# Two conv-gated FFNs: five column groups of seven block products instead of four, each beside a narrow group, and two weight sums made by DMA

## The chip, the cores and the metric

The kernel runs on one core of one Trainium2 chip. The metric is device microseconds of one execution, as the median of some runs of the same program. Five engines of the core work side by side, each through its own queue of instructions in order: TensorE (PE, with its weight loads shown apart as PEld), VectorE (DVE), ScalarE (ACT), GpSimd (POOL) and SyncE (SP, which here only issues DMAs). They wait for each other through semaphores. TensorE reads SBUF and writes PSUM, which this kernel uses as eight banks of 512 fp32 columns per partition.

## The reference

Two decoder layers over 256 positions of width 2048. Each has a token mixer (layer 0: dilated attention in three groups; layer 1: stick-breaking attention on a shared K/V; both beside cross-attention into 256 memory tokens) and then a gated MLP with a causal depthwise convolution of width 3 on the gate branch. The change touches the MLP alone:

```python
def _conv_ffn(h, w_up, w_conv, b_conv, w_down):      # w_up 2048 x 11264, w_down 5632 x 2048
    u = h @ w_up
    gate, val = jnp.split(u, 2, axis=-1)
    gp = jnp.pad(gate, ((0, 0), (CONV_WIDTH - 1, 0), (0, 0)))
    acc = b_conv + gp[:, CONV_WIDTH - 1:CONV_WIDTH - 1 + S] * w_conv[CONV_WIDTH - 1]
    for j in range(CONV_WIDTH - 1):
        acc = acc + gp[:, j:j + S] * w_conv[j]
    return (jax.nn.silu(acc) * val) @ w_down
...
    f = _conv_ffn(_rmsnorm(x, norms[2]), w_up, w_conv, b_conv, w_down)
    return x + _rmsnorm(f, norms[3])
```

## The kernel before

**Arithmetic.** Every fp32 matrix is split into a high and a low part of the type fp32r: ACT casts the high part (`hi`, L557), DVE subtracts it to get the low part (`lo`, L558). A product is then three matmuls, hi·hi, lo·hi and hi·lo (`mm3`). Weights come as pieces of 1 MB (128 x 2048) into the ring `raw` (3 buffers), and each half of a piece takes a buffer of the rings `whi` and `wlo` (4 each).

**The FFN** (`ffn`, called for layer 0 and layer 1) walks over the 5632 columns of the gate and of the value in 11 groups of 512, each group twice 512 columns of `w_up`.

- A *narrow* group is eight tiles of 128 columns (`ws_pair`, `ws_tile`): weights stationary, the activations h moving, 16 matmuls of 512 columns (L135, L138) and 16 of 256 (L136) into one bank `ps_g`. An ACT copy (L139) and a DVE add (L140) empty the bank. Then the gate is scaled by the row factor R (L743), convolved (ACT L712, DVE L715), put through SiLU (L717), multiplied with the value (L727), and split (L253, L254).
- A *wide* group (`wide`, groups 2, 4, 6 and 8) makes gate and value together as a 2 x 2 block product with seven products instead of eight (a Strassen-Winograd form): token halves by rows, even and odd k-tiles, gate and value columns. It runs over eight *units* of k. One unit needs a 1 MB piece of weights, four sums of its quarters (DVE L590, L591, L592), splits of both, and 7 x 3 matmuls of 512 columns into seven banks that stay open over all units: products 1, 2, 6, 7 in `ps_g`, products 3, 4, 5 in `ps_s`. One bank of `ps_s` is left. Sums of the activations (`sums_of_h`, its step `make`) are made once per FFN. The results come out with tokens on partitions, and `turned` turns them by sixteen transposes (L758).
- The *down* product of a group is four pieces, each 24 matmuls (`as_mm`). In the wide stage one down piece is put beside the seven products of each unit: its first half ahead of products 1, 2, 3, its second half between them and products 7, 5, 6, 4. It uses the one free `ps_s` bank twice, and ACT alone empties it (L701). The partial results go by accumulating DMA from the POOL queue into `yout` in DRAM (L689).

**What sets the order.** Instructions are scheduled by a planner, except those under `pin` while `self.pinned` is true: each of those is kept behind the one that was written before it on its engine. Inside `wide`, PE, ACT and DVE thus follow the program text. `later(n, fn)` hangs a step on the n-th weight piece from now.

The activation rings that matter are `sh` (11 buffers of 4 KB per partition) and `qk` (5). The tile `x` serves as the residual and, during the wide groups, as room for the split sums (`forms`); the residual waits in DRAM (`xout`).

Of the kernel before, what the change touches and what calls it, by code (L numbers as in the profile page):

```python
# [36 lines left out]
WIDE = (2, 4, 6, 8)  # L37
# [8 lines left out]
class Body:  # L46
    def __init__(self, ctx, tc, a):
        self.tc, self.nc, self.a = tc, tc.nc, a
        self.sb = ctx.enter_context(tc.tile_pool(name="sb", bufs=1))
        self.todo = []  # L50
        self.pinned = False
        self.psp = ctx.enter_context(tc.tile_pool(name="ps", bufs=1, space=bass.MemoryType.PSUM))
        self.outside = ctx.enter_context(tc.tile_pool(name="outside", bufs=1, space=bass.MemoryType.DRAM))
# [28 lines left out]
    def step(self):  # L82
        if self.todo:
            for fn in self.todo.pop(0):
                fn()

# [54 lines left out]

    def ws_pair(self, src, h, out=None, before=None, R=None):
# [25 lines left out]
    def as_piece(self, banks, src, lhs, pi, cuts=1, between=None):  # L168
        self.step()
        parts = self.piece(src[pi], cuts, between=between and between[0])  # L170
# [23 lines left out]
    def rstd(self, ss):  # L194
# [5 lines left out]
        nc.gpsimd.tensor_tensor(r, v, self.mhalf[:, 0:n], op=ALU.pow)  # L200
        return r
# [50 lines left out]
    def split_heads(self, src, hi, lo):  # L252
        self.nc.scalar.copy(hi, src)  # L253
        self.nc.vector.tensor_sub(lo, src, hi.bitcast(F32))  # L254
# [281 lines left out]
    def sums_of_h(self, h):  # L536
# [3 lines left out]
        nc = self.nc  # L540
        s = self.sb.tile([P, KT // 2, 4, 2, P], F32R, name="h1", tag="h1", bufs=1)

        def make(i):
            a, d = self.pairtile(), self.pairtile().rearrange("p a (b t) -> p (a b) t", b=2)
            hh = h[2][:, 2 * i:2 * i + 2, :, :].bitcast(F32)
            nc.vector.tensor_add(a, hh[:, :, 0, :], hh[:, :, 1, :])
            a1, a2 = a[:, :, 0:P], a[:, :, P:S]
            nc.vector.tensor_add(d[:, 0, :], a2[:, 0, :], a2[:, 1, :])
            nc.vector.tensor_sub(d[:, 1, :], d[:, 0, :], a1[:, 0, :])
            nc.vector.tensor_sub(d[:, 2, :], a1[:, 0, :], a2[:, 0, :])  # L550
            nc.vector.tensor_sub(d[:, 3, :], a1[:, 1, :], d[:, 1, :])
# [8 lines left out]
    def wide(self, src, h, s, forms, r, downs):  # L560
# [9 lines left out]
        pin, sub = self.pin, nc.vector.tensor_sub  # L570
# [11 lines left out]
        def load(u):  # L582
            raw = self.sb.tile([P, 2048], F32, name="raw", tag="raw", bufs=3)
            nc.sync.dma_start(raw, src[u])
            return raw

        def sums(raw):

            d, e = self.sh([P, 1024]), self.sh([P, 1024])
            pin(sub(d, raw[:, 1024:], raw[:, 512:1536]))  # L590
            pin(sub(half(e, 1), half(raw, 3), half(d, 0)))  # L591
            pin(sub(half(e, 0), half(raw, 0), half(e, 1)))  # L592
            return d, e

        def plain(raw):
# [3 lines left out]
            self.split(*(half(f, 0) for f in fb), half(raw, 3))  # L599
            return fa, fb  # L600

        summed = [[forms[:, 2 * i + j, :] for j in range(2)] for i in range(2)]
        def split_sums(t):
            for of, parts in zip(t, summed):
                self.split(*parts, of)

        raw = load(0)
        t = sums(raw)
        split_sums(t)
        d = downs[0]()  # L610
        next(d)
        f = plain(raw)
        self.pinned = True
        for u in range(n):
            more = u + 1 < n
            next(d)
            if u:
                split_sums(t)
            next(d)
# [4 lines left out]
            if more:  # L624
                raw = load(u + 1)
                t, f = sums(raw), plain(raw)
            next(d)
# [8 lines left out]
            d = after  # L636
        a = [self.sc([P, 512]) for _ in range(2)]
        g0, v1 = self.sc([P, 512]), self.sc([P, 512])
        rt = [r[:, t:t + 1] for t in range(2)]
        for t in range(2):  # L640
            pin(nc.scalar.activation(a[t], ps[1], AF.Copy, scale=rt[t]))  # L641

        def add(out, i, t, to):
            pin(nc.vector.scalar_tensor_tensor(out, ps[i], rt[t], to, op0=ALU.mult, op1=ALU.add))

        add(g0, 2, 0, a[0])
        add(a[1], 7, 1, a[1])
        add(a[0], 6, 0, a[0])
        add(a[1], 6, 1, a[1])
        add(v1, 5, 1, a[1])  # L650
        add(a[0], 5, 0, a[0])
        add(a[0], 3, 0, a[0])
        add(a[1], 4, 1, a[1])
        self.pinned = False
        return (g0, a[1]), (a[0], v1)

    def ffn(self, layer, h, each, filler=None, done=None, late=None):
# [3 lines left out]

        def rms():
            with self.tc.issue_after(self.last_hi.ins):
                rx = self.x_rstd()
            R.append(rx)
# [11 lines left out]
        for i in range(KT // 2):  # L677
            self.later(2 * i + 1, lambda i=i: make(i))
# [3 lines left out]
        ss = self.sums(2)  # L682
        acts = {}

        def out(g, c, part):
            if g == 0:
                nc.gpsimd.dma_start(yout[c], part)
            else:
                nc.gpsimd.dma_start(yout[c], part, accum_op=ALU.add)  # L689

        def down(g, c):


            parts = self.piece(dn[c, g])
            y = self.sh([P, 1024])
            yield
            for t in range(2):
                b = self.bank("s")
                self.as_mm([b, b], parts, acts[g], 0, (t,))
                yield  # L700
                self.pin(nc.scalar.copy(y[:, t * 512:(t + 1) * 512], b))  # L701
                if t:
                    out(g, c, y)
                else:
                    yield

        def conv(p, ga):
            c = self.pairtile()
            for j in range(2):
                ft = 2 * p + j  # L710
                w = [self.cols[:, cv + i * NFT + ft:cv + i * NFT + ft + 1] for i in range(4)]
                nc.scalar.activation(c[:, j, :], ga[:, j, :], AF.Identity, scale=w[2], bias=w[3])  # L712
# [361 lines left out]
```

## Time and profile before

| | |
|---|---|
| median of 3 runs | 2205.47 us (2205.09 to 2206.46) |
| profiled execution | 2204.65 us, span of the profile 2202.9 us |
| clock granted to TensorE | 0.999 |
| DMA | 470.65 MB, mean 214 GB/s |
| wide groups | 64 units (two FFNs x 4 groups x 8) |

Times in the profile are in microseconds from the start of the span. A line such as L558 is a line of the kernel; a helper's line stands for all its callers, so tiles (`raw`, `sh`, `qk`) tell the stages apart. In a timeline a matmul's length runs to its modelled end; the distance between two starts is what it costs the engine. Names stand as out<-in.

### The profile page before, as it was taken

What the parts mean: (1) busy time and instruction counts of PE and PEld (TensorE: products, weight loads), DVE (VectorE), ACT (ScalarE), POOL (GpSimd) and SP (SyncE); (2) the same over time, 40 slices, a digit from 0 to 9 for tenths busy, and PEclk for the clock granted to TensorE, in tenths of its full rate; (3) what the DMA queues carried; (4) which work ended last, traced back from release to release, by engine and by line L of the source; (5) the groups of instructions that cost most, each with busy time, mean ns of one, the idle gap of its engine ahead of it and who ended that gap; (6) DMA issues with size and microseconds to landing.
All of it is one profiled execution on the core that took longest, in us unless ns stands there. A gap on an engine that the chain in (4) does not pass through costs nothing.

```text
span 2202.9 us, 29043 instructions
## 1 busy us (share of the span) xinstructions
PE 2188.7 (99%) x11106; PEld 1848.0 (84%) x11106; DVE 1713.0 (78%) x2215; ACT 1297.1 (59%) x1838; POOL 79.9 (4%) x122
## 2 busy tenths in 40 slices
PE   9999999999999999999999999999999999999998
PEld 7888888888888888888888888878888888888886
DVE  6566767898888989886674667568989889898766
ACT  7545656666565666665464545456666666666543
POOL 0000000000000000010000000000000000001000
PEclk9999999999999999999999999999999999999999
DMA  8755556557586786886555444555685868768753
GB/s 316 268 181 179 184 172 210 191 210 249 191 259 211 235 238 210 251 302 208 188 172 191 144 173 171 183 195 194 223 254 190 259 196 247 229 213 257 278 191 133
DMA packets 73708, 470.65 MB, mean 214 GB/s; under 512 B 8416, under 2 KB 8800, under 8 KB 23008
## 3 DMA queue, kind: packets, MB, share of 16 engines
q1 hardware_dynamic: 60768, 418.45, 55.2%
q0 software_dynamic: 12800, 50.34, 9.5%
q8 instruction: 87, 1.43, 0.3%
q14 instruction: 53, 0.43, 0.0%
HBM read 428.91 MB, written 39.85 MB: 213 GB/s over the span
## 4 chain that ended last, share of the span: by engine, by line
PE 98%; issue 1%; DVE 1%; DMA 0%; ACT 0%; SPq 0%; POOLq 0%; POOL 0%; DVEq 0%; ACTq 0%
PE ps_g L135 28%; PE ps_g L118 26%; PE ps_s L118 23%; PE ps_g L136 15%; PE ps_g L138 2%; PE ps_s L758 1%; PE ps_s L240 1%; DMA raw<-in_wmv_dram 0%; PE ps_s L291 0%; PE ps_s L318 0%; DVE wlo L558 0%; PE ps_s L397 0%; PE ps_s L354 0%; PE ps_s L455 0%; PE ps_s L415 0%
## 5 line engine op out<-in xcount | busy, mean ns | idle before, releaser
L558 DVE TENSOR_TENSOR wlo<-raw,whi 128x1024 fp32r<-128x1024 f32 (+1 forms) x758 | 881.3, 1174 | 328.8 <-ACT whi L557 316.2
L557 ACT CAST whi<-raw 128x1024 fp32r<-128x1024 f32 (+1 forms) x758 | 760.5, 1012 | 395.2 <-PE ps_g L118 166.5
L135 PE MATMUL ps_g<-h,whi 128*128 128x512 f32 x2640 | 943.0, 399 | 0.2 <-DVE h L230 0.2
L136 PE MATMUL ps_g<-h,wlo 128*128 128x256 f32 x2816 | 761.0, 280 | 0.0
L135 PEld LDWEIGHTS ps_g<-h,whi 128*128 128x128 f32 x2640 | 495.8, 188 | 114.6 <-ACT sc L641 1.9
L136 PEld LDWEIGHTS ps_g<-h,wlo 128*128 128x128 f32 x2816 | 531.6, 189 | 14.2
L118 PE MATMUL ps_s<-whi,sh 128*128 128x512 f32 x1088 | 336.6, 391 | 0.0
L118 PE MATMUL ps_g<-whi,h 128*128 128x512 f32 x816 | 254.1, 392 | 0.9 <-ACT whi L557 0.9
L118 PEld LDWEIGHTS ps_s<-whi,sh 128*128 128x128 f32 x1088 | 204.4, 188 | 45.2
L118 PE MATMUL ps_s<-wlo,sh 128*128 128x512 f32 x544 | 214.3, 394 | 0.4 <-DVE wlo L558 0.4
L139 ACT COPY qk<-ps_g 128x256 f32<-128x256 f32 x160 | 59.4, 371 | 209.1 <-PE ps_g L138 209.0
L118 PEld LDWEIGHTS ps_g<-whi,h 128*128 128x128 f32 x816 | 152.7, 188 | 34.8 <-ACT whi L557 1.3
L118 PE MATMUL ps_g<-whi,sh 128*128 128x512 f32 x560 | 174.8, 393 | 0.0
L558 DVE TENSOR_TENSOR x<-sh,x 128x1024 fp32r<-128x1024 f32 x128 | 156.2, 1223 | 18.5 <-ACT x L557 11.4
L118 PE MATMUL ps_g<-wlo,h 128*128 128x512 f32 x408 | 160.2, 393 | 0.2
L557 ACT CAST x<-sh 128x1024 fp32r<-128x1024 f32 x128 | 134.4, 1050 | 17.4 <-PE ps_s L118 16.4
L701 ACT COPY sh<-ps_s 128x512 f32<-128x512 f32 x128 | 74.4, 581 | 106.0 <-PE ps_s L118 106.0
L118 PEld LDWEIGHTS ps_g<-whi,sh 128*128 128x128 f32 x560 | 104.8, 188 | 22.1
L118 PEld LDWEIGHTS ps_s<-wlo,sh 128*128 128x128 f32 x544 | 102.2, 188 | 23.2 <-DVE wlo L558 1.3
L140 DVE TENSOR_TENSOR qk<-ps_g,qk 128x256 f32<-128x256 f32 x160 | 67.3, 420 | 55.2 <-ACT qk L139 54.4
L118 PE MATMUL ps_g<-wlo,sh 128*128 128x512 f32 x280 | 109.8, 392 | 0.0
L118 PE MATMUL ps_g<-x,h 128*128 128x512 f32 x384 | 109.2, 392 | 0.0
(173 smaller groups left out, 1953.9 us busy)
## 6 DMA issues: line engine op xcount, KB each, us to landing
raw<-in_up_dram SPq DMA_DIRECT2D x112, 1024.0 KB, 5.0
raw<-in_dn_dram SPq DMA_DIRECT2D x88, 1024.0 KB, 4.8
raw<-in_uw_dram SPq DMA_DIRECT2D x64, 1024.0 KB, 7.2
yout<-sh POOLq DMA_DIRECT2D x64, 512.0 KB, 8.4
raw<-in_wqk_a_dram SPq DMA_DIRECT2D x24, 1024.0 KB, 4.8
raw<-in_wo_b_dram SPq DMA_DIRECT2D x16, 1024.0 KB, 4.9
raw<-in_wv_a_dram SPq DMA_DIRECT2D x12, 1024.0 KB, 4.9
raw<-in_wv_b_dram SPq DMA_DIRECT2D x12, 1024.0 KB, 4.8
```

The costliest lines, as they stand in the source:

```text
L118: mm = lambda *o, **k: self.pin(self.nc.tensor.matmul(*o, **k))
L135: mm(b, whi[:, ks], both, start=kt == 0, stop=False)
L136: mm(b[:, 0:S], wlo[:, ks], one, start=False, stop=False)
L138: mm(b, whi[:, ks], both, start=False, stop=True)
L139: nc.scalar.copy(out, b[:, S:])
L140: nc.vector.tensor_add(out, b[:, 0:S], out)
L240: self.nc.tensor.transpose(b[:, k * S + t * P:k * S + (t + 1) * P], self.x[:, t, kt * P:(kt + 1) * P], self.ident)
L557: self.pin(self.nc.scalar.copy(hi, of))
L558: self.pin(self.nc.vector.tensor_sub(lo, of, hi.bitcast(F32)))
L701: self.pin(nc.scalar.copy(y[:, t * 512:(t + 1) * 512], b))
L758: nc.tensor.transpose(b[:, j * S + t * P:j * S + (t + 1) * P], of[t][:, f:f + P], self.ident)
```

## The change

Groups 1, 3, 5, 7 and 9 of each FFN are wide now, five instead of four. Beside the products of each unit stands one tile of the *narrow* group behind it (`ws_beside`, `beside`: eight tiles beside eight units), where a down piece stood. The two down products of earlier groups (`downs`) come between wide groups as a stage of their own. What belongs to the narrow tiles (gate, convolution, product, splits) is put into a list (`behind_this`) of which one step is taken at each of two places of a unit (`catch_up`). Of the four weight sums of a unit, two that lie in one buffer `d` are made by DMA: a load of two quarters, and on top of it an accumulating DMA from the POOL queue that adds the fourth quarter to both. DVE makes the other two. The signs of the activation sums change with it, and `turned` goes through an ACT copy. Three of the eight `make` steps move into the first wide group. The last three down products keep their place at the end, with the wide group's own last.

```diff
-WIDE = (2, 4, 6, 8)
+WIDE = (1, 3, 5, 7, 9)
...
+    def catch_up(self, n=1):
+        while self.behind and n:
+            self.behind.pop(0)()
+            n -= 1
...
+    def ws_beside(self, out, src, h, done=None):
+        parts = self.piece(src)
+        yield
+        b = self.bank("s")
+        mm = lambda *o, **k: self.pin(self.nc.tensor.matmul(*o, **k))
+        for half, (whi, wlo) in enumerate(parts):
+            for k in range(8):
...
+                if kt < KT - 1:
+                    mm(b, whi[:, ks], both, start=kt == 0, stop=False)
+                mm(b[:, 0:S], wlo[:, ks], one, start=False, stop=False)
+                if kt == KT - 1:
+                    mm(b, whi[:, ks], both, start=False, stop=True)
+            yield
+        self.pin(self.nc.scalar.copy(out, b[:, S:]))
+        self.pin(self.nc.vector.tensor_add(out, b[:, 0:S], out))
+        if done:
+            done()
...
-        def sums(raw):
-            d, e = self.sh([P, 1024]), self.sh([P, 1024])
-            pin(sub(d, raw[:, 1024:], raw[:, 512:1536]))
-            pin(sub(half(e, 1), half(raw, 3), half(d, 0)))
-            pin(sub(half(e, 0), half(raw, 0), half(e, 1)))
-            return d, e
+        def first_sums(u):
+            d = self.sh([P, 1024])
+            nc.sync.dma_start(d, src[u][:, 512:1536])
+            nc.gpsimd.dma_start(d.rearrange("p (a n) -> p a n", a=2),
+                                src[u][:, 1536:].unsqueeze(1).to_broadcast([P, 2, 512]), accum_op=ALU.add)
+            return d
+        def sums(d, raw):
+            e = self.sh([P, 1024])
+            pin(add(half(e, 1), half(d, 0), half(raw, 2)))
+            pin(add(half(e, 0), half(e, 1), half(raw, 0)))
+            return d, e
...
         for u in range(n):
             more = u + 1 < n
-            next(d)
+            next(b)
             if u:
                 split_sums(t)
-            next(d)
+            self.catch_up()
             fa, fb = f
             product(1, u, fa, 1)
             product(2, u, fa, 0)
             product(3, u, fb, 0)
             if more:
                 raw = load(u + 1)
-                t, f = sums(raw), plain(raw)
-            next(d)
+                if u + 2 < n:
+                    ahead.append(first_sums(u + 2))
+                t, f = sums(ahead.pop(0), raw), plain(raw)
+            self.catch_up()
+            next(b)
             if more:
-                after = downs[u + 1]()
+                after = beside[u + 1]()
                 next(after)
-            next(d, None)
+            next(b, None)
             product(7, u, summed[0], 1)
             product(5, u, summed[0], 0)
             product(6, u, summed[1], 1)
             product(4, u, summed[1], 0)
...
+        def downs(groups):
+            lhs = [p for b in groups for p in acts[b]]
+            for c0 in (0, 2):
+                banks = {c: [self.bank(), self.bank()] for c in (c0, c0 + 1)}
+                for pi, b in enumerate(groups):
+                    for c in banks:
+                        self.as_piece(banks[c], dn[c, b:], lhs, pi, at=0)
...
+        def beside(g):
+            st = {}
+            def tile(p, i, j):
...
+                def first():
+                    gate(ga)
+                    st["c"], st["shifted"] = conv(p, ga)
+                def product():
+                    st["parts"] = keep(p, st["c"], val)
+                done = None
+                if j == 1:
+                    done = (lambda: self.behind_this(first, lambda: st["shifted"]())) if i == 0 else (
+                        lambda: self.behind_this(product, lambda: st["parts"]()))
+                return self.ws_beside(st[p][i][:, j, :], up[place(p), i][j], h, done)
...
         narrow(0)
-        narrow(1)
-        before = [0, 1]
+        self.behind_this(*(lambda i=i: make(i) for i in range(5, KT // 2)))
         for g in WIDE:
-            downs = [lambda b=b, c=c: down(b, c) for b in before for c in range(4)]
-            made = self.wide(uw[WIDE.index(g)], h, s, forms, R[0], downs)
+            made = self.wide(uw[WIDE.index(g)], h, s, forms, R[0], beside(g + 1))
             for i in range(2):
                 self.later(2 + i, lambda made=made, g=g, i=i: turned(g, made, i))
-            narrow(g + 1)
-            before = [g, g + 1]
-        narrow(GROUPS - 1)
+            if g < WIDE[-1]:
+                downs((max(g - 2, 0), g + 1))
```

`first` is the scaling of the gate and the two ACT identities of `conv`; `shifted` is the four DVE multiply-adds of the convolution and SiLU on ACT; `product` and `parts` are the product with the value and its split. All of them are pinned when they are taken inside `wide`.

More of the change, by code (lines that the diff above doesn't have):

```diff
@@ L676, in ffn @@
         self.later(1, rms)
-        for i in range(KT // 2):
-            self.later(2 * i + 1, lambda i=i: make(i))
+        for i in range(5):
+            self.later(i + 2, lambda i=i: make(i))
         cv = COL_CONV + layer * 4 * NFT
         yout = self.outside.tile([4, P, 1024], F32, name="yout", tag="yout", bufs=1)
-        ss = self.sums(2)
         acts = {}
[L685 to L689, printed above, removed]
```

219 lines of the change are left out of this document (121 added, 98 removed).

## The prediction

> **What bounds the kernel now.** I read the engine totals first, then the chain that ended last, then stages of the feed-forward block, and at last single queues.
>
> ```profile
> PE 2188.7 (99%) x11106; PEld 1848.0 (84%) x11106; DVE 1713.0 (78%) x2215; ACT 1297.1 (59%) x1838; POOL 79.9 (4%) x122
> PE 98%; issue 1%; DVE 1%; DMA 0%; ACT 0%; SPq 0%; POOLq 0%; POOL 0%; DVEq 0%; ACTq 0%
> ```
>
> TensorE has work in 99% of the span, and 98% of the chain is its own. So matmul columns are the currency, and a saving elsewhere is worth nothing by itself. The 78% of VectorE is an average over stages. In five units of a wide group, seen as one window (columns: window, length, then busy time and count of PE, PEld, DVE, ACT, POOL; clock; DMA share; GB/s), it looks like this:
>
> ```profile
> 492.88:544.52 51.64, 51.64 (x227) 42.26 (x226) 44.34 (x43) 33.73 (x41) 3.65 (x5) 1.00 0.77 248
> ```
>
> A unit takes 51.64/5 = 10.33 us and PE never pauses. VectorE is at 86%, so this stage has little room. That it fits comes from the order on the queues, seen in one such unit by three timelines, of PE, ACT and DVE (start, length, engine, line):
>
> ```profile
> 656.24 0.39 PE L118 MATMUL ps_s<-whi,sh 128*128 128x512 f32 x1
> 656.70 0.86 PE L118 MATMUL ps_g<-x,h 128*128 128x512 f32 x3
> 659.45 0.39 PE L118 MATMUL ps_s<-whi,sh 128*128 128x512 f32 x1
> ...
> 656.67 1.05 ACT L557 CAST whi<-raw 128x1024 fp32r<-128x1024 f32 x1 [0.32 <-PE ps_s L118]
> 657.63 0.57 ACT L701 COPY sh<-ps_s 128x512 f32<-128x512 f32 x1
> ...
> 651.36 1.22 DVE L590 TENSOR_TENSOR sh<-raw 128x1024 f32<-128x1024 f32 x1
> 652.62 0.69 DVE L591 TENSOR_TENSOR sh<-raw,sh 128x512 f32<-128x512 f32 x1
> 653.34 0.69 DVE L592 TENSOR_TENSOR sh<-raw,sh 128x512 f32<-128x512 f32 x1
> 654.31 1.83 DVE L558 TENSOR_TENSOR wlo<-raw,whi 128x1024 fp32r<-128x1024 f32 x2 [0.27 <-ACT whi L557]
> 656.38 2.60 DVE L558 TENSOR_TENSOR wlo<-raw,whi 128x1024 fp32r<-128x1024 f32 x2 [0.25 <-ACT whi L557]
> ```
>
> Products 7, 5, 6, 4 run from 656.70 to 659.45: 12 matmuls in 2.75 us, 0.229 us each. The cast of the second half of the next weights waits for the buffer that the last matmul before them read (656.24 + 0.39, cast at 656.67). Behind it ACT empties the one free ps_s bank, done at 658.20. The next matmul into that bank is due at 659.45, so the hand-over has 1.25 us to spare, and VectorE has no part in it.
>
> **The change, part by part.** *Matmul columns.* Per block, one more group of the eleven becomes wide. What leaves is eight narrow tiles, one of which lasts from 399.23 to 404.86; what comes is 8 x 21 matmuls and sixteen transposes.
>
> ```profile
> 399.23 0.48 PE L135 MATMUL ps_g<-h,whi 128*128 128x512 f32 x1
> 404.86 0.39 PE L135 MATMUL ps_g<-h,whi 128*128 128x512 f32 x1
> ...
> 561.92 1.04 PE L758 MATMUL ps_s<-ident,sc 128*128 128x128 f32 x8
> 562.71 0.48 PE L135 MATMUL ps_g<-h,whi 128*128 128x512 f32 x1
> ```
>
> 8 x 5.63 = 45.0 leaves; 168 x 0.229 = 38.5 and 2 x 0.79 = 1.6 come. That is 4.9 us less per block, **9.8 us** for two. The down projection keeps its 24 matmuls per piece wherever it stands.
>
> *What stands beside the seven products.* A unit was 21 + 24 matmuls (10.33 us). It becomes 21 plus a narrow tile, 4.81 + 5.63 = 10.44 us: half the tile (2.8), products 1 to 3 (2.06), the other half (2.8), products 7, 5, 6, 4 (2.75). The tile has one bank for both halves, since products 3, 4, 5 hold the other three ps_s. It is emptied by an ACT copy and then a VectorE add, and both are pinned *behind* the splits of the next tile's weights. I follow the new wait with these rows:
>
> ```profile
> L140 DVE TENSOR_TENSOR qk<-ps_g,qk 128x256 f32<-128x256 f32 x160 | 67.3, 420 | 55.2 <-ACT qk L139 54.4
> L712 ACT ACTIVATE qk<-qk,cols 128x256 f32<-128x256 f32 x56 | 30.7, 595 | 5.3 <-DVE qk L743 5.3
> L715 DVE SCALAR_TENSOR_TENSOR qk<-qk,cols 128x255 f32<-128x255 f32 x56 | 24.6, 477 | 0.0
> L717 ACT ACTIVATE qk<-qk 128x512 f32<-128x512 f32 x44 | 27.7, 631 | 8.2 <-DVE qk L715 8.1
> L743 DVE TENSOR_TENSOR qk<-qk,R 128x512 f32<-128x512 f32 x28 | 19.3, 689 | 0.6
> ...
> 469.26 0.50 PE L118 MATMUL ps_s<-wlo,sh 128*128 128x512 f32 x1 [0.21 <-DVE wlo L558]
> 469.60 0.63 PE L118 MATMUL ps_s<-whi,sh 128*128 128x512 f32 x2
> ```
>
> Count from E, the start of product 7. In a narrow tile the last matmul is the one that reads whi, so the buffer is free at E - 0.23 + 0.40. With 0.04 for a hand-over (656.63 to 656.67), the cast ends at E + 1.26. VectorE starts its subtract at E + 1.30. Independent instructions follow each other a little faster than they last (654.31: 1.22 + 0.69 done in 1.83), so the add starts 1.15 later and ends at E + 2.87. PE wants the bank at E + 2.75. It starts at 2.93, and the first matmul after a wait takes 0.34 in place of 0.23 (469.26 to 469.60). So **0.29 us** per hand-over. Queued behind the add is the next unit's split of the sums; who waits is PE, with everything behind it.
>
> *The narrow group's own elementwise work* now enters the pinned queues, one step at each of two places in a unit. In units 2 and 6 both steps come: the gate scaling with two ACT identities, then four shifted multiply-adds with SiLU. SiLU is pinned on ACT ahead of the next tile's casts, and it waits for VectorE. From the previous add's end on, VectorE's path is: two subtracts of the sums, the second behind its cast, 2.4; gate 0.69; then two identities (2 x 0.5) and a cast (1.05) on ACT before the plain subtracts can run, with hand-overs 2.1 (the two DVE sums of 0.69 fit in there); plain subtracts 1.15 + 0.62; four multiply-adds 1.9; SiLU and the next cast, 0.6 + 1.05 + hand-overs 0.1, with VectorE idle; two subtracts 2.3; the add 0.42. That is 13.3, and 13.2 from add to add, against 10.44: **2.8 us** in each of two units. Unit 4 carries only the product (0.69) and its split (a cast and 0.68), which fits. A wide group has seven hand-overs: 5 x 0.29 + 2 x 2.8 = 7.0 us. Ten groups: 70 us. In each block's first group three steps that make activation sums come too:
>
> ```profile
> L548 DVE TENSOR_TENSOR qk<-qk 128x128 f32<-128x128 f32 x16 | 4.5, 281 | 0.0
> L546 DVE TENSOR_TENSOR qk<-h 128x512 f32<-128x512 f32 x16 | 10.9, 683 | 0.0
> L253 ACT CAST h<-qk 128x512 fp32r<-128x512 f32 x16 | 9.9, 618 | 2.7 <-DVE qk L551 2.7
> ```
>
> One costs 0.68 + 4 x 0.28 + 0.70 + 0.68 = 3.2 us of VectorE's path. Two stand in unit 0, which has no split of sums: 6.4 + 1.4 + 1.8 + 2.3 + 0.4 = 12.3. With half a microsecond in unit 1, I take 2.3 us per block beyond the 7.0. **Waits in all: 70 + 4.6 = 75 us.**
>
> Bounds of these waits: without hand-over times and restart, 0.1 x 50; and if SiLU did not stand before the casts, 1.1 x 20, together 27. If the plain casts wait for their old buffer (after product 2, as they do now), 3.3 x 20 + 0.4 x 50 + 7 = 93. I take 75, as every duration in it has a row.
>
> *Two of the four sums by DMA.* This removes a VectorE subtract of 1.22 per unit. That is real, but VectorE's idle time is in the wrong place for it to matter. What it adds are an SP load of 512 KB and a POOL accumulation from rows of 2 KB into SBUF, for which no row exists. The nearest are the accumulations into yout, in the window of the first wide group (queue: packets, MB, share of 16 engines over 83 us):
>
> ```profile
> q1 hardware_dynamic: 2339, 17.06, 59.0%
> q0 software_dynamic: 1008, 3.67, 16.3%
> yout<-sh POOLq DMA_DIRECT2D x8, 512.0 KB, 8.2
> ...
> L689 POOL DMA_DIRECT2D yout<-sh x56: 842/850/887, 518.6 to 2035.0; - x56
> L584 SPq DMA_DIRECT2D raw<-in_uw_dram x64: 327/328/328, 447.4 to 2004.5; - x64
> ```
>
> A yout packet (4 KB) takes 0.163 x 1328/1008 = 0.215 engine-us; loads move 21.8 kB per engine-us. Per unit 2.36 MB of loads are 6.8 us of the sixteen engines. The 256 accumulating packets are 1.7 us if they cost by bytes, 3.4 us if each costs a yout packet: 8.5 to 10.2 us in a unit of 10.44. So DMA is near its limit but not over it; I take nothing. Latency: the load and the accumulation are issued two units ahead (some 20 us) against 5 + 8 us. The Trainium skill (DMA: Bandwidth & Descriptors, Anatomy of one DMA — SWDGE (gpsimd) path) fits 2.0 us plus bytes by 436 kB/us; for 512 KB that would be an estimate of 3.2 us where the trace has 8.2, which leaves the term at nothing either way. The measured 8.2 counts.
>
> *Moved or small, taken as nothing:* the down pieces between the groups (5.5 us of PE each against 2.4 of VectorE); half as many yout accumulations; ACT copies of the transposed results, in that stage, where ACT is half idle; the last pieces and the evacuation at a block's end, in nearly the same order. If that cover went, I would expect 0 to 2 us per block. POOL issues 16 + 40 DMAs per block where it issued 32 (0.85 us each), SP 40 more (0.33 each), and neither is on the path.
>
> **Sum.** The profiled execution took 2204.65 us (span 2202.9; the median of the runs is 2205.47, 0.8 higher). 2204.65 - 9.8 + 75 = 2269.9; on the median's footing **2270 us**, about 3% slower.
>
> **Rivals.** (a) *Only the bank's hand-over bites*, and SiLU hides: 70 x 0.29 = 20 us, so 2215. For it: ACT is at 65% in this stage. Against: the pinned order has no gap for it. (b) *Faster*: the tile's bank is free in time. Then the matmul columns alone speak: 2196. It decides at 9.8/70 = 0.14 us per hand-over. For it speaks that VectorE's work per unit does not grow (1.22 goes, 1.4 comes) and that there is no pause now. Against it stands the addition above, 2.93 against 2.75, before any elementwise step. (c) *The DMA sums come late*, so the change does not relieve VectorE but makes it wait. If an accumulating packet cost 0.43, a unit would need 6.8 + 6.9 = 13.7 us: 80 x 3.3 = 260 us more, 2460. The point is 0.23 per packet; yout's 0.215 is close below, but for twice the bytes.
>
> **Numbers.** Forecast 0.62 (its own bounds: 2222 to 2288), (a) 0.14, (b) 0.14, (c) 0.06, waits that just cancel the saving 0.04. The range 2207 to 2300 leaves out (b), most of (c) and the cancelling case. About 0.2% (4.4 us) is what a measurement can tell here: faster 0.14, within 0.04, slower 0.82.
>
> **What would show it.** Right: in wide groups PE waits for the add that empties the narrow tile (the evacuation in ws_beside), about 70 times, with units of 10.7 us and two of some 13 us per group; ACT waits for the shifted multiply-adds before SiLU, and DVE for the casts behind it. Wrong: units of 10.44 us throughout (b), two long units missing (a), DVE waiting for DMA at the adds of the sums (c), or waits at the seams between groups, which I took as nothing.

## The result, and the profile after

The changed kernel takes **2406.57 us** (median of 4 runs, 2404.74 to 2408.47) against 2205.91 us before. The ratio is 1.091, with a 95% interval of 1.0891 to 1.0929: 200.7 us slower. The forecast was 2270 us, with a range of 2207 to 2300. So the sign was right, and the excess is three times the one forecast (201 us against 65).

The engine totals and the chain that ended last, of the changed kernel (2403.0 us of span):

```profile
PE 2249.9 (94%) x10962; PEld 1867.8 (78%) x10962; DVE 1657.3 (69%) x2175; ACT 1302.3 (54%) x1844; POOL 148.6 (6%) x168
...
q1 hardware_dynamic: 72288, 439.43, 52.4%
q0 software_dynamic: 29952, 75.51, 15.5%
...
PE 82%; DMA 7%; DVE 6%; issue 3%; ACT 2%; SPq 0%; DVEq 0%; POOL 0%; POOLq 0%; ACTq 0%
```

TensorE's own work is 82% of the chain where it was 98%. DMA alone is now 7% of 2403 us, some 170 us, and it was 0%. TensorE's busy time has also grown by 61 us though there are 144 matmuls and transposes fewer, so matmuls have become slower somewhere. The view of waits says who waits for whom (engine, line, what it waited for; us in total, times, longest):

```profile
PEld ps_s L156 <- DVE qk L169: 106.5, 70, 6.2
DVE sh L636 <- DMA sh<-in_uw_dram: 98.5, 10, 13.3
...
ACT qk L765 <- DVE qk L763: 78.5, 30, 3.3
PE ps_s L156 <- DVE qk L169: 77.0, 30, 5.8
...
ACT x L593 <- DMA sh<-in_uw_dram: 67.8, 10, 9.0
```

The first row is the hand-over of the narrow tile's bank (L169 is the add that empties it), 70 times as forecast. The second was the forecast's sign for rival (c): the adds of the sums (L636) wait for DMA, exactly once per wide group.

I took the length of each of the 80 units from TensorE's timeline, from the first matmul of one unit's narrow tile to that of the next one's (for the last unit, to the end of its products). One middle group of the first FFN, its eight units in us, and the first group of that FFN; the other runs are described below (10.44 is the unit without any wait by the sum of the prediction):

| kernel | middle group, units 0 to 7 | first group, units 0 to 7 |
|---|---|---|
| the change | 24.67, 12.24, 13.02, 10.67, 10.79, 10.68, 13.01, 10.57 | 19.53, 12.85, 13.02, 10.72, 10.73, 10.67, 13.02, 10.56 |
| all sums on VectorE | 10.86, 10.67, 13.42, 12.17, 10.78, 10.66, 13.41, 12.13 | 20.36, 13.43, 13.42, 12.03, 10.79, 10.73, 13.42, 12.12 |
| SiLU apart | 24.31, 12.19, 10.78, 10.79, 10.73, 10.72, 10.79, 10.61 | 19.28, 12.88, 10.78, 10.73, 10.74, 10.66, 10.78, 10.56 |
| bank emptied early | 23.68, 12.14, 12.00, 10.56, 10.50, 10.50, 11.99, 10.61 | 18.10, 13.20, 12.00, 10.55, 10.50, 10.50, 12.00, 10.61 |
| SiLU and bank | 23.21, 10.57, then 10.5 | 18.66, 12.87, then 10.5 |
| all three edits | 10.45, then 10.5 | 19.24, 13.12, then 10.5 |
| the last version | 10.45, then 10.5 | 11.30, then 10.5 |

Units 2 to 7 of the change are as forecast (10.73, and 13.2 for units 2 and 6) in most groups; unit 3 takes 12.2 us in three of the ten groups and unit 7 12.1 in four. Over the ten groups the eight positions exceed 10.44 us by 119 us in unit 0, 22 in unit 1, 52 in units 2 and 6, and 20 in the other four. That is 213 us, or 203 with the 9.8 us of columns saved; 201 were measured. Unit 0 alone holds more than half.

Here is the start of that middle group, as timelines of SP, POOL, DVE, ACT and PE show it (start, length, engine and line; in brackets the idle time before and what ended it):

```profile
718.62 0.33 SPq L107 DMA_DIRECT2D raw<-in_up_dram  x1
719.04 1.91 SPq L628 DMA_DIRECT2D sh<-in_uw_dram  x3
...
729.96 1.21 POOL L629 DMA_DIRECT2D sh<-in_uw_dram  x1 [5.94 <-DMA sh<-in_uw_dram]
...
736.66 0.69 DVE L636 TENSOR_TENSOR sh<-sh,raw 128x512 f32<-128x512 f32 x1 [13.34 <-DMA sh<-in_uw_dram]
...
736.65 1.04 ACT L593 CAST x<-sh 128x1024 fp32r<-128x1024 f32 x1 [8.96 <-DMA sh<-in_uw_dram]
...
737.75 1.22 PE L127 MATMUL ps_g<-x,h 128*128 128x512 f32 x2 [8.11 <-ACT x L593]
```

The load into `d` is issued at 719.04, 2.8 us before unit 0 begins (721.82): SP issues in order, and from 700 to 722 it stood twice, 9.2 us in all, for VectorE to free a buffer of `raw` for the narrow tile's weights. POOL waits until it has landed and starts to accumulate onto it 10.9 us after the issue; the result is there at 736.65, **17.6 us** after the issue. VectorE wanted it at 723.32 (736.66 - 13.34), so the real lead was 4.3 us. ACT splits it, and product 7 of unit 0 starts after 8.1 us of idle TensorE. VectorE stands for 13.3 us in its fixed order, with the next narrow tile's split behind it. The windows of that stretch (window, length, busy time and count of PE, PEld, DVE, ACT, POOL; granted clock; DMA share; GB/s), and its queues from 719.04 to 758.80:

```profile
721.82:737.70 15.88, 7.83 (x42) 6.46 (x40) 2.50 (x4) 4.84 (x7) 4.48 (x4) 0.86 1.03 259
737.75:746.50 8.75, 5.78 (x13) 3.65 (x13) 8.29 (x11) 4.20 (x5) 0.34 (x1) 0.67 1.01 278
746.50:758.80 12.30, 12.30 (x54) 10.11 (x54) 8.23 (x10) 5.18 (x7) 2.04 (x2) 0.86 1.01 295
758.80:772.00 13.20, 10.96 (x54) 8.94 (x55) 10.62 (x15) 8.03 (x11) 1.19 (x1) 1.00 0.85 236
```

```profile
q1 hardware_dynamic: 1440, 7.34, 54.2%
q0 software_dynamic: 1432, 3.26, 46.1%
...
sh<-in_uw_dram SPq DMA_DIRECT2D x6, 512.0 KB, 9.3
sh<-in_uw_dram POOLq DMA_DIRECT2D x5, 512.0 KB, 6.7
```

Two things stand in these rows. The sixteen DMA engines are full (1.01 to 1.03) for the first 37 us of the group. The packets of POOL's queue, nearly all of them of the accumulations with 2 KB each, cost 0.461 x 636/1432 = 0.205 us; so my upper bound (a yout packet's 0.215 for half the bytes) was close to the true price here. (In the window 738 to 820, where the engines aren't always full, the same sum gives 0.234 x 1312/1709 = 0.180.) And the clock granted to TensorE falls to 0.67 after the pause: unit 1 has no wait inside 746.50 to 758.80 (PE is busy throughout), but takes 12.30 us for 54 matmuls, where 53 make a unit of 10.44 us. The mean granted clock in it is 0.86, and 12.30 x 0.86 is 10.6.

### The profile page after: what moved, and what is told of

It reads as the page before. It is cut to its first block, busy times and chain, and to the rows that moved or that the text cites. A ratio compares the mean times of both kernels' runs of the same rounds, so it can differ in the third digit from the quotient of the medians.

```text
span 2403.0 us, 29033 instructions
## 1 busy us (share of the span) xinstructions
PE 2249.9 (94%) x10962; PEld 1867.8 (78%) x10962; DVE 1657.3 (69%) x2175; ACT 1302.3 (54%) x1844; POOL 148.6 (6%) x168
## 4 chain that ended last, share of the span: by engine, by line
PE 82%; DMA 7%; DVE 6%; issue 3%; ACT 2%; SPq 0%; DVEq 0%; POOL 0%; POOLq 0%; ACTq 0%
PE ps_g L127 35%; PE ps_s L156 18%; PE ps_g L144 11%; PE ps_s L127 8%; DMA sh<-in_uw_dram 6%; PE ps_g L145 6%; DVE wlo L594 3%; ACT whi L593 1%; PE ps_s L848 1%; PE ps_g L147 1%; PE ps_s L272 1%; DVE qk L169 1%; DVE qk L763 1%; DMA raw<-in_up_dram 0%; DVE x L594 0%
## 5 line engine op out<-in xcount | busy, mean ns | idle before, releaser
L156 PE MATMUL ps_s<-h,whi 128*128 128x512 f32 x1280 | 495.7, 421 | 77.1 <-DVE qk L169 77.0
L127 PE MATMUL ps_g<-whi,sh 128*128 128x512 f32 x1488 | 464.3, 393 | 0.0
L144 PE MATMUL ps_g<-h,whi 128*128 128x512 f32 x1200 | 430.7, 401 | 0.2 <-DVE h L262 0.2
L156 PEld LDWEIGHTS ps_s<-h,whi 128*128 128x128 f32 x1280 | 254.5, 199 | 161.9 <-DVE qk L169 106.5
L156 PE MATMUL ps_s<-h,wlo 128*128 128x256 f32 x1280 | 359.9, 291 | 3.1 <-DVE wlo L594 3.1
L145 PE MATMUL ps_g<-h,wlo 128*128 128x256 f32 x1280 | 346.3, 281 | 0.0
L127 PE MATMUL ps_g<-wlo,sh 128*128 128x512 f32 x744 | 291.9, 392 | 0.0
L144 PEld LDWEIGHTS ps_g<-h,whi 128*128 128x128 f32 x1200 | 225.5, 188 | 51.5 <-DVE h L262 0.7
L156 PEld LDWEIGHTS ps_s<-h,wlo 128*128 128x128 f32 x1280 | 256.2, 200 | 11.4 <-DVE wlo L594 4.0
L145 PEld LDWEIGHTS ps_g<-h,wlo 128*128 128x128 f32 x1280 | 241.9, 189 | 6.3
```

What stands on the lines that cost most here:

```text
L127: mm = lambda *o, **k: self.pin(self.nc.tensor.matmul(*o, **k))
L144: mm(b, whi[:, ks], both, start=kt == 0, stop=False)
L145: mm(b[:, 0:S], wlo[:, ks], one, start=False, stop=False)
L156: mm = lambda *o, **k: self.pin(self.nc.tensor.matmul(*o, **k))
```

## The experiments

All runs are compared with the change (2406.6) and with the kernel before on the same chip (2204.9 to 2206.7). A run without a range is one execution. Three theories stood at first: S, that the sums by DMA come too late in unit 0 of each group, since their loads stand behind other loads on SP; R, that unit 0 is late anyway at the seam, by buffers or by the down pieces' weights; and C, that the DMA engines can't carry the accumulations.

**1. All four sums on VectorE.** The load takes the whole 1 MB again.

```diff
         def first_sums(u):
+            return None
...
         def sums(d, raw):
+            if d is None:
+                d = self.sh([P, 1024])
+                two = lambda v: v.rearrange("p (a n) -> p a n", a=2)
+                pin(add(two(d), two(raw[:, 512:1536]), half(raw, 3).unsqueeze(1).to_broadcast([P, 2, 512])))
```

> As the changed kernel, but VectorE makes all four weight sums (the whole 1 MB piece is loaded; no load into d, no accumulating DMA). Theory S: the first unit of each wide group is long (18.5 to 24.7 us) because its sums by DMA come late, the loads into d standing on SP behind the second unit's weights. Then the first units go to 10.7 us (12.6 in each block's first group), the second units lose the slow clock (12.3 to 10.7), units 2 and 6 grow by 0.3 for the extra subtract, and the time is 2196 + 85 = about 2280 us. Rival R: the seam between groups is long for another reason (buffers, the down pieces' weights). Then first units stay above 18 us and the time stays within 40 us of 2407.

Measured: 2320.8 us, 86 less. Unit 0 falls from 24.67 to 10.86 in the middle groups. So S holds for eight groups of ten, and in unit 0 VectorE did not need the relief. Two things were not foreseen: unit 0 of each FFN's first group stays at 20.4 us, and units 3 and 7 take about 12.2 us in nearly every group, behind units 2 and 6 that are 0.4 us longer.

**2. The sums of units 0 and 1 alone on VectorE** (as above, with `if u < 2`).

> As the changed kernel, but the sums of units 0 and 1 of each group are made by VectorE; units 2 to 7 keep the DMA sums. Theory S (late only at the start of a group): first units 10.7 us, time 2196 + 75 = about 2270 us. Rival C (the sixteen DMA engines cannot carry the accumulation): the wait moves to units 2 and 3, VectorE waits there for DMA, and the time stays above 2350 us.

Measured: 2329.5. Unit 0 is 10.9 us in the middle group, but units 1 and 2 grow there (13.47 and 13.51): the sums of unit 2, which are now the first by DMA, come late as well. The result lies between the two forecasts (2270, and above 2350). S is right about unit 0, but moving two units is not enough: the wait moves and VectorE still waits for DMA, as C said, though for less time.

**3. The first two sums issued earlier,** half-way through the down stage ahead of the group.

```diff
+                if c0:
+                    self.ahead = [self.first_sums(then, u) for u in range(2)]
```

> As the changed kernel, but in eight of the ten groups the first two loads into d and their accumulations are issued half-way through the down stage before the group, ahead of the group's own weights on SP. Nothing else differs. Theory S, in the form that the place on the SP queue is the cause: first units of these eight groups fall from 21 to 25 us to 10.7 to 12, second units to 10.7; 8 x 13.5 less, about 2300 us. If instead the accumulating DMA is slow in itself (rival C), less than half of that goes.

Measured: 2372.7, only 34 less. Unit 0 is 10.6 us in the groups with the edit, so lateness of `d` was what made it long. But the wait moves: units 1 and 2 rise to 16.34 and 13.66 in the middle group (`d` of unit 2 is late), and the down stage ahead gets some 5 us longer (50.4 us from the end of one group at 665.50 to the next at 715.88; 45.7 in the change). There ACT, in its fixed order, stands for `d` of unit 0 ahead of the casts of the down pieces' weights, and TensorE then waits for these:

```profile
706.13 1.04 ACT L593 CAST x<-sh 128x1024 fp32r<-128x1024 f32 x1 [10.37 <-DMA sh<-in_uw_dram]
...
708.17 0.97 PE L127 MATMUL ps_g<-whi,sh 128*128 128x512 f32 x2 [2.28 <-ACT whi L593]
```

This load was issued at 686.05, so the pair took 20.1 us here. The expectation asked for at least half of 8 x 13.5 us if the place on the SP queue is the cause, and 34 us are less; so it is a part of the cause at most. With a DMA share of 0.96 (715.88 to 742.80) an earlier issue moves the wait.

**4. SiLU as a step of its own,** so that it stands a place later on ACT's fixed order.

```diff
-                    done = (lambda: self.behind_this(first, lambda: st["shifted"]())) if i == 0 else (
+                    done = (lambda: self.behind_this(
+                        first, lambda: st["shifted"]((0,), False), lambda: st["shifted"]((1,), False),
+                        lambda: st["shifted"](()))) if i == 0 else (
```

> As the changed kernel, but the four shifted multiply-adds and SiLU are three steps instead of one (two multiply-adds, two multiply-adds, SiLU), taken one at a place. Theory Q: units 2 and 6 are long (13.0 us) because both elementwise steps and SiLU stand ahead of the next tile's splits; they go to 10.7 us, 20 x 2.3 = 46 us less, about 2360 us. Rival: these units are long for VectorE's amount of work over the group or for the lowered clock; then the time moves by less than 15 us, the long units only shifting to units 3 and 7.

Measured: 2357.7, 49 less, with units 2 and 6 at 10.73 to 10.80 (one of the twenty at 11.07). So these two units are long because of the steps that stand ahead of the next tile's casts, as forecast. The edit spreads the multiply-adds over two places as well, so what SiLU's own place costs isn't separated.

**5. The narrow tile's bank emptied early:** the copy and the add stand between the two splits of the next tile's weights, where in the change they stand behind both.

```diff
             next(b, None)
+            if more:
+                next(after)
             product(7, u, summed[0], 1)
```

(`ws_beside` then splits one half of its weights per step.)

> The change, but the ACT copy and the VectorE add that empty the narrow tile's bank stand ahead of the split of the second half of the next tile's weights (in the change behind it). The sums by DMA and SiLU's place stay. Theory B (the hand-over of the one bank costs the 0.28 us by which units 3, 4 and 5 are longer than 10.44): those units become 10.44 to 10.5 us, the waits of the first matmul of product-like tiles for the add (70 x 1.5 us in the change's view of waits) mostly go, and the whole is 15 to 25 us shorter, 2382 to 2392. Rival (the units are longer for another reason, such as the restart of the matmul pipeline or the weights): the units stay at 10.7 and the whole stays within 8 us of 2406.

Measured: 2347.9, 59 less. Units 4 and 5 become 10.50 as expected, but the gain is more than twice the one expected. Units 2 and 6 lose 1.0 us each too (20 us in all), units 3 and 7 no longer have slow matmuls (12 us), units 0 and 1 are shorter by some 20 us. I had counted the five plain hand-overs only.

**6. All three edits** (1, 4 and 5 together).

> Three edits at once: all four weight sums on VectorE, SiLU and the shifted multiply-adds spread over three steps, and the narrow tile's bank emptied ahead of the second split. Theory (the three costs are separate and add up): units of 10.44 to 10.9 us in all places but the first unit of each block's first wide group (which stays near 20 us for another reason), so the whole is 2196 (the columns alone) + 2 x 10 for these first units + about 10 of rests = 2215 to 2235, still 0.5 to 1.3% above the kernel before. Rival (VectorE, which now has 1.22 us more in each unit, becomes the bound): units of 11.2 us or more, 80 x 0.8 = 64 us above the columns, so 2270 or more. A result below 2205 would say that the first units' 20 us were part of the same cause.

Measured: **2218.5** (2218.16 to 2219.02), ratio 1.0052 (1.0034 to 1.007). Nearly every unit is 10.45 to 10.5 us, but not the first two of each FFN's first group: 19.24 and 13.12, and 19.27 and 12.24. The single gains add up to nearly this (86 + 49 + 59 = 194 against 188), but that is partly luck: pair by pair they do not (see 12). Outside the first groups VectorE is no bound.

**7. The same, with only units 0 and 1 summed on VectorE.**

> As the kernel with three edits, but only the sums of units 0 and 1 of a group are on VectorE, the others by DMA as in the change. If the DMA sums of units 2 to 7 come late only because their loads stand behind those of the weights of a group's start, units 1 and 2 stay long (11.7 to 15 us, as when only those two were moved) and this is 20 to 60 us slower than the kernel with all four sums on VectorE; if VectorE is the bound, it is faster than that one.

Measured: 2244.2, 26 more. Units 1 and 2 are long again (12.66 and 12.13 in the middle group). In the last group of that FFN, which begins at 957.35, SP, POOL and DVE have these rows for unit 2's sums:

```profile
954.54 0.42 SPq L635 DMA_DIRECT2D sh<-in_uw_dram  x1
...
964.78 1.21 POOL L636 DMA_DIRECT2D sh<-in_uw_dram  x1 [5.22 <-DMA sh<-in_uw_dram]
...
976.49 0.69 DVE L647 TENSOR_TENSOR sh<-sh,raw 128x512 f32<-128x512 f32 x1 [5.97 <-DMA sh<-in_uw_dram]
```

From issue to use are 21.95 us, more than two units of 10.5, with the load alone taking 10.2. The DMA share in these two units is 1.02 and 0.99. The load is issued 2.8 us before unit 0, and unit 1 still waits for it: at this duration even a lead of two units would not do.

**8 and 9. The first group of each FFN.** What is left above 10.5 us sits in it, 11.4 and 10.9 us per FFN. Theory V: VectorE has more work than time there. Ahead of the first wide group is now only one narrow group (45 us), in which it must also make five of eight activation sums, and three more follow in the wide group. Theory W: the first weights are late. A window of the kernel with three edits, ahead of the late unit and into it:

```profile
400.00:430.00 30.00, 27.44 (x151) 23.50 (x150) 29.52 (x54) 19.14 (x28) 0.00 (x0) 0.95 0.40 134
```

VectorE is busy for 29.52 of 30 us, and DMA at 0.40. I tried two remedies: the additions of `make` on POOL (seven operations for each step there in place of five), and the three late `make` steps at every other place.

> As the kernel with three edits, but the additions and subtractions of all eight steps that make the activation sums (make) are on the POOL queue, which is nearly idle there; only the low part of the split (0.68 us each) stays on VectorE. Theory V (the 8.8 us by which unit 0 of each block's first wide group is too long, and most of the 2 us of unit 1, are VectorE's overload: about 54 us of its work for 45 us of the only narrow group ahead of it): unit 0 falls from 19.2 to 10.5 - 12 us in both blocks, and the whole from 2218.5 to 2196 - 2204, below the kernel before. Rival W (it is the first weights' transfer and the ring raw that are late): unit 0 stays near 19 us, and the whole at 2212 or more. If POOL's operations are slow beyond 10 us per step, both blocks' first groups wait for POOL and the whole is above 2218.

> As the kernel with three edits, but the three make steps that stand in the first wide group are put at every other place instead of at successive ones, so two stand in unit 0 no longer. Theory V (overload of VectorE by amount): the overload stays and only moves; unit 0 is 2 to 4 us shorter, units 1 and 2 as much longer, the whole within 6 us of 2218.5. Rival (only their standing together costs): the first groups lose 8 us or more each, 2203 or less. Theory W (late transfers): no change of unit 0 at all.

On POOL: 2229.2 (2227.72 to 2229.84), 11 *more*. Unit 0 is 22.34 us. The reason is in POOL's timeline, two operations of one form and size, with VectorE's rows beside them:

```profile
374.98 0.47 POOL L587 TENSOR_TENSOR qk<-qk 128x128 f32<-128x128 f32 x1
...
425.86 5.52 POOL L587 TENSOR_TENSOR qk<-qk 128x128 f32<-128x128 f32 x1
...
374.92 3.23 DVE L267 SCALAR_TENSOR_TENSOR h<-ps_s,cols,h 128x256 fp32r<-128x256 f32 x8 [0.62 <-ACT h L266]
...
425.84 0.68 DVE L647 TENSOR_TENSOR sh<-sh,raw 128x512 f32<-128x512 f32 x1
426.44 2.35 DVE L598 TENSOR_TENSOR wlo<-raw,whi 128x1024 fp32r<-128x1024 f32 x2
...
430.98 0.42 DVE L149 TENSOR_TENSOR qk<-ps_g,qk 128x256 f32<-128x256 f32 x1
```

VectorE is busy beside both. POOL's operation takes 0.47 us beside instructions that read PSUM (`ps_s`). It takes 5.52 us beside additions and subtractions of two tensors in SBUF, and ends at 431.38, when VectorE has turned to a tensor in PSUM. Its step takes 13 us (421.36 to 434.4), ACT waits 10.0 us for POOL's results (from 415 to 446), and the whole is above 2218, as the expectation said for a step of more than 10 us. VectorE loses too. Four shifted multiply-adds in this kernel, and in the one with three edits:

```profile
422.28 2.70 DVE L776 SCALAR_TENSOR_TENSOR qk<-qk,cols 128x255 f32<-128x255 f32 x4
```

```profile
416.74 1.66 DVE L777 SCALAR_TENSOR_TENSOR qk<-qk,cols 128x255 f32<-128x255 f32 x4
```

So this run does not separate V from W. At every other place: 2214.8, 3.7 less; units 0 to 2 are 15.84, 12.24, 12.23. The overload has mostly moved, as V says; W, by which nothing would change, falls.

**10. The last version** removes work from VectorE there, not only its clusters: in each FFN's first group the sums of units 2 to 7 are by DMA, the late `make` steps begin at unit 1 and are cut in two, and the earlier five start a weight piece sooner.

```diff
-            self.later(i + 2, lambda i=i: make(i))
+            self.later(i + 1, lambda i=i: make(i))
...
-        self.behind_this(*(lambda i=i: make(i) for i in range(5, KT // 2)))
+        steps = [lambda: None] * 2
+        for i in range(5, KT // 2):
+            steps += [lambda i=i: fin.__setitem__(i, make(i, True)), lambda i=i: fin[i]()]
+        self.behind_this(*steps)
...
-            made = self.wide(uw[WIDE.index(g)], h, s, forms, R[0], beside(g + 1))
+            made = self.wide(uw[WIDE.index(g)], h, s, forms, R[0], beside(g + 1),
+                             2 if g == WIDE[0] else 8)
```

> As the kernel with three edits (2218.5), but in each block's first wide group the two sums of d are by DMA from unit 2 on (1.22 us of VectorE less in each of six units), the three make steps there are taken from unit 1 on and in two halves, and the five make steps in the narrow group ahead start one weight piece sooner. Theory V (overload of VectorE by amount, about 11 us per block): the slack so made is 7.3 us in the first wide group and some 3 us ahead of it, so the first groups fall from 95 to 85 - 89 us and the whole to 2198 - 2208, level with the kernel before. Rival (the accumulating DMAs come late here too): units 1 and 2 stay at 12 us or more, the first groups at 91 us or more, the whole at 2211 or more.

Measured: **2198.72** (8 runs, 2197.69 to 2199.56), ratio 0.9971 (0.996 to 0.9982): faster than the kernel before by 6.4 us, or 0.3%. Unit 0 of the first groups is 11.30 and 11.22 us, all others are 10.45 to 10.50. Its first group, units 0 to 4 (columns as above):

```profile
422.58:433.90 11.32, 10.82 (x55) 8.79 (x54) 11.20 (x15) 6.46 (x10) 0.00 (x0) 1.00 0.92 269
433.90:444.40 10.50, 10.50 (x55) 8.85 (x54) 10.40 (x16) 6.53 (x9) 1.60 (x2) 1.00 1.02 307
444.40:454.90 10.50, 10.50 (x55) 8.85 (x54) 10.40 (x16) 6.47 (x9) 0.79 (x1) 1.00 0.99 278
454.90:465.40 10.50, 10.50 (x55) 8.84 (x54) 10.40 (x17) 6.46 (x9) 2.37 (x2) 1.00 1.01 288
465.40:475.90 10.50, 10.50 (x55) 8.85 (x54) 9.62 (x13) 6.83 (x10) 0.64 (x1) 1.00 0.98 293
```

VectorE is at 99% in four of these five units and DMA at 92 to 102%, and TensorE never pauses after unit 0. The DMA sums come in time here although DMA is full. The issue of the first load, and the add that needs it:

```profile
414.66 0.42 SPq L638 DMA_DIRECT2D sh<-in_uw_dram  x1
...
438.59 0.69 DVE L650 TENSOR_TENSOR sh<-sh,raw 128x512 f32<-128x512 f32 x1
```

That is a lead of 23.9 us, since the load goes out 7.9 us before unit 0 (422.58) and the sums of the first two units are VectorE's; the DMA share ahead of it, from 400 to 414, is 0.39. The DMA sums take work from VectorE in a place where it has too much. Three things were changed at once, so which of them gave how much isn't known.

**11 and 12. SiLU and bank, the sums by DMA kept** (4 and 5 together).

> The change with two edits, SiLU taken as a step of its own and the narrow tile's bank emptied ahead of the second split; the sums by DMA stay. If the costs are separate and add up, the gains of the two single edits add: 2406.6 - 48.9 - 58.7 = 2299, with units of 10.5 us from 2 to 7 and only units 0 and 1 long. If they share a cause, 2320 or more. All that is then left above the kernel before (some 94 us) is the sums by DMA, unit 0 and 1 of each group.

> The kernel with SiLU as a step of its own and the bank emptied early, once more: in its first execution (4472 us) matmuls took 0.68 us where they take 0.39 in all other runs, from the start to the end, and the profile gave no granted clock. If that was that execution's, the sum of the two single gains stands to be seen now: 2299 if the costs are separate, 2320 or more if they share a cause. If it belongs to the kernel, it is 4470 again.

The first execution took 4472 us and is no measure of the kernel: it ran with every matmul at little more than half speed. The groups of TensorE's largest line (mean ns behind the busy time) in it, and then in the second run:

```profile
L161 PE MATMUL ps_s<-h,whi 128*128 128x512 f32 x1280 | 846.8, 673 | 8.5 <-DVE qk L174 8.5
```

```profile
L161 PE MATMUL ps_s<-h,whi 128*128 128x512 f32 x1280 | 477.3, 408 | 24.6 <-DVE qk L174 22.0 <-ACT whi L598 2.5
```

The second time the kernel took 2320.3 (4 runs, 2313.35 to 2327.03). Units 2 to 7 are 10.5, so the forecast's part of the loss is gone, and only units 0 and 1 are long. The two gains together are 86 us where their sum is 108, since both edits remove the same waits of units 2 and 6 and the same slow matmuls behind them. What is left is this wait (total, times, longest), which the run with all three edits can't have, as it makes no sum by DMA:

```profile
DVE sh L641 <- DMA sh<-in_uw_dram: 106.0, 11, 13.3
```

By taking the sums back to VectorE one comes from here to 2218.5: with everything else in place, **the sums by DMA cost 102 us** (86 where they are taken back first, as in experiment 1).

## Why the prediction was wrong

From the change to the last version there are three steps with a price each: 2406.6 - 86.3 (hand-over and SiLU) - 101.8 (sums by DMA) - 19.8 (the first groups) = 2198.7. Against the forecast:

- **Matmul columns, 9.8 us less.** The last version is 6.4 us below the kernel before, with units of 10.50 instead of 10.44 (80 x 0.06 = 5 us). The rest fits within the interval of the ratio (4 to 9 us).
- **Hand-over of the bank, and SiLU ahead of the casts: 70 us.** Right in mechanism (70 hand-overs; mostly 10.67 to 10.79 and 13.02 us where 10.73 and 13.2 were forecast; both edits remove what they should). The two edits give back 86 us, of which a part is what no step of mine had: slow matmuls after pauses.
- **The first group's activation sums: 4.6 us for two blocks.** 20 us. The term counted the two `make` steps in unit 0 on an idle VectorE. But VectorE arrives there late: the one narrow group ahead has no room for the other five, and unit 0 inherits that.
- **Sums by DMA, taken as nothing.** 102 us; this is the step that failed: "the load and the accumulation are issued two units ahead (some 20 us) against 5 + 8 us". Where the loop runs evenly the step was right. In the middle group of the change the adds of units 2 to 7 come 22.9 to 28.6 us after the issue of their load, and none waits. For unit 3:

```profile
738.55 0.51 SPq L628 DMA_DIRECT2D sh<-in_uw_dram  x1
...
761.47 0.68 DVE L636 TENSOR_TENSOR sh<-sh,raw 128x512 f32<-128x512 f32 x1
```

It fails at the start of a group, twice. There are no two units ahead: the lead was 4.3 us, so even 5 + 8 us would have come 8.7 us late. And 5 + 8 are latencies of a DMA that isn't full: the pair takes 17.6 us (21.95 in the run with two sums on VectorE), which makes 8.7 into the 13.3 of VectorE's wait. I had bounded a unit's need at 8.5 to 10.2 us of 10.44 and concluded "near its limit but not over it". The price per packet came near the upper one, and the share is 1.01 for 37 us; that the queue drains slowly because of that price is my reading, not a separate run. Rival (c) had the sign right (VectorE waits for DMA at the adds) and the price wrong: packets cost 0.18 to 0.205, not 0.43, and less than the 0.23 from which a unit would have had too much of them.
- **Seams between the groups: 0 to 2 us per block.** The down stage itself is no longer than in the last version (45.7 us from the last product of a group to the next group in both); the loss that I named there as a sign of being wrong sits in unit 0, behind the seam.
- **Clock.** No step had it. In the change TensorE's mean granted clock is 0.969, and in the last version 0.999. With the waits gone it is gone, so it comes with them (the rows are in the last section); no run kept the waits without the slow matmuls, so its share isn't known by itself.

Term by term the forecast was short by some 102 us (sums by DMA), 15 (first groups), 16 (hand-over and SiLU) and 3 (columns): 136 us together, where measured and forecast differ by 137. The waits that were forecast give the right sign, but less than half of the loss.

What stays open: whether one more buffer would let the sums by DMA come in time. No run has a larger ring `sh`.

## What to carry to other kernels

A lead time counted in steady-state units does not hold at the start of a loop: look at what is issued when the first pass begins, and at what else is in the DMA queues then. When a resource comes out at 0.8 to 1.0 of its time by your own bounds, "not over" is no reason to take its latency from an idle stretch. Work taken from an engine is worth something only where that engine is late: the same DMA sums cost 102 us in all groups, and stand in a version that beats both kernels where VectorE is overloaded and the loads have a lead. What they gave there by themselves was not measured.

## What was not expected of the hardware

- **Pauses make the matmuls behind them slow.** In the kernel with all sums on VectorE, TensorE stands idle for 2.6 to 2.7 us in units 2 and 6, and in 19 of 20 cases the next unit takes 12.0 to 12.3 us. Three windows, with such a pause at the end of the first (columns as above):

```profile
742.00:749.70 7.70, 5.09 (x26) 3.94 (x24) 5.93 (x10) 4.33 (x6) 0.00 (x0) 0.99 0.42 138
749.70:753.00 3.30, 3.27 (x10) 2.79 (x11) 3.30 (x3) 0.35 (x1) 0.00 (x0) 0.50 0.77 261
753.00:756.00 3.00, 3.00 (x17) 2.52 (x16) 2.18 (x4) 1.59 (x2) 0.00 (x0) 1.00 0.15 63
```

The granted clock is 0.50 for 3.3 us, and full again behind it. In the change the pauses in units 2 and 6 are 2.2 to 2.3 us, and 7 of 20 next units are slow; with the bank emptied early they are 1.3 us (one 1.6), and none is. The Trainium skill (TensorE: Matmul & The Clock Gate, What's actually happening) tells of a window of about 3.4 us that runs freely, after which an idle TensorE has half its clock until as long a stretch of work has passed. The half clock and its length agree; pauses shorter than that window sufficed here, and not in each group.
- **Matmuls can stay at little more than half speed.** One kernel ran its whole 4472 us with matmuls of 673 ns in place of 408, and the granted clock showed nothing (1.00). The same kernel took 2320 us the next time. No row says why.
- **POOL and VectorE disturb each other.** A 128x128 subtraction on POOL takes 0.47 us beside a VectorE that reads PSUM, and 5.52 beside one that takes two tensors from SBUF for as long; VectorE's own multiply-adds grow from 1.66 to 2.70 us for four. A busy VectorE is thus not enough to slow POOL; what it reads seems to decide, which no run tested by itself.
- **An accumulating DMA into SBUF with 2 KB runs** costs 0.18 to 0.205 us of an engine per packet, where one with 4 KB into DRAM cost 0.215: half the bytes save a sixth at most.
